# Passages between sub-layers of a two-layer decoder trunk: from the scheduler's order to a written one

## The chip, the cores and the metric

The kernel runs on one core of a Trainium2 chip. The metric is the device time of one execution in microseconds (us). TensorE (PE) multiplies matrices, VectorE (DVE) and ScalarE (ACT) do the work per element, GpSimd (POOL) only small powers here, and SyncE (SP) issues the transfers from the chip's memory.

## The reference, cut to what matters

Two layers; in each a mixing sub-layer and a channel sub-layer on x of 256 tokens by 1024 columns, in f32:

```
mod = silu(c) @ w_ada + b_ada            # shift, scale, gate for both sub-layers
h   = rmsnorm(x) * (1 + scale1) + shift1
q,k,v (two attentions), gate_A, gate_B = split(h @ w_in)
y   = (sigmoid(gate_A) * W_oA(swa(q,k,v)) + sigmoid(gate_B) * W_oB(moba(q,k,v))) @ w_out
x   = x + gate1 * y
h   = rmsnorm(x) * (1 + scale2) + shift2
x   = x + gate2 * (relu(h @ w_up)**2 @ w_down)      # 1024 -> 4096 -> 1024
```

## The kernel before, in words

**Three products for one.** Every f32 operand is split into a high part (a cast to the matrix engine's fp32r format) and a low part (the rest), and every product is three: high by high, high by low, low by high (L523, L524, L525 where the weights are streamed, L528 to L530 where they stand still). A product here is one instruction of 128x128 by 512 columns.

**Weights.** `Stream` (from L387) loads pieces of 2x1024 columns into three raw buffers (`wraw`), ahead of time and in the order of use. Each half of a piece is split into one of eight slots (four `w`, and `ahi`, `alo`, `qT`, `kv`, which attention uses at other times): ACT casts the high part (L441), DVE subtracts it for the low part (L447). A slot comes free when its last product is issued. `fill` splits into every free slot; `stream.hold` stops ordinary splits; with the word "later" the cast is issued and the subtraction kept on a list.

**Sums for the conditioning.** `mod` is not a product on PE: DVE adds up rows of `w_ada` (L257, L260, tile `ada`; 140 long additions L260 in all) as work in the background that `tick()` lets forward a step at a time.

**A passage** lies between two sub-layers. There are three: mixing to channel in layer 0 (near 204 us), channel of layer 0 to mixing of layer 1 (near 392 us), mixing to channel in layer 1 (near 564 us). `out_product` holds its last two blocks of columns back: 48 products, which are then done in four quarters of twelve, token tile t by column half h, so that each quarter of the sum is complete early. A quarter's sum goes through `residual` on DVE (L660 times the gate, L661 onto `x_sb`). When both halves of a token tile are there, `ln_stats` forms the norm: ACT squares and sums (L542, two instructions and a read of the sum each), DVE adds (L545, `lnr`), POOL takes the power (L546), DVE scales x by it (L553, two halves, tile `ln`). `ln_apply(t, h)` then takes four of the eight 128-column blocks: PE transposes them (L571), ACT and DVE each scale and shift two (L578, L581), DVE and ACT round to the high part (L588, L590), DVE subtracts for the low part (L591, two instructions). In the text, half (t, h) is such a half of a token tile.

**After the passage's products**, `proj_first` computes the first 512 columns of the next projection, for token tile 0 and then tile 1, from four weight slots in order, six products each: slots one and two take half (t, 0), slots three and four half (t, 1). The next work is the rest of that projection, or in the channel sub-layer the up-products (L633, L637) with `uhi` and `ulo` (L1253, L1259) as the split of the activated rows.

**The order.** The tile framework's scheduler decides where on each engine an instruction stands, within its data dependences; `tc.issue_after` adds edges, which `stream.behind` uses to put weight splits behind the last `ln_apply`. A block under `tc.manual_schedule()` keeps the written order instead. The lead of layer 0 already uses it. Names with a number are one allocation of a buffer.

Of the kernel before, what the change touches and what calls it, by code (L numbers as in the profile page):

```python
# [8 lines left out]
F32 = mybir.dt.float32  # L9
# [9 lines left out]
DEPTH = 2  # L19
# [42 lines left out]
HOLD = 2  # L62
PAIR_TICKS = 3
ROPE_LAG = 3
XN_ACT = ()
G_LAG = 2
PACE = 2
SM_ACT = ((0, 1, 2, 3), (3,))
# [11 lines left out]
def kernel(ctx: ExitStack, tc: tile.TileContext, io):  # L80
# [102 lines left out]
    def run(g):  # L183
        for _ in g:
            pass
# [204 lines left out]
    class Stream:  # L390
# [58 lines left out]
            if h == 1:  # L449
                self.load_next()  # L450

        def fill(self):
            n = -1
            while n != self.split:
                n = self.split
                self.split_next()

# [205 lines left out]
    def out_product(n, us, make, n0, lsub, after):  # L663
# [16 lines left out]
                held += [(f, k) for k in range(2)]  # L680
        while slow:
            run(slow.pop(0))
        stream.fill()
        stream.hold = True
        halves = []
        for t in range(NT):
            for h in range(2):
                for i, (f, k) in enumerate(held):
                    if t == 0 and h == 0:
                        halves.append(stream.get())  # L690
                    while us[f][2][0] > 0:
                        tick()
                    out_half(accs, halves[i], *us[f], k, f == 0 and k == 0, i == len(held) - 1, (t,), (h,))
                    if t == 0 and h == 0:
                        tick()
                    if t == 1 and h == 1:
                        stream.release(halves[i][0])
                    if i == 1:
                        after(t, h, 0, lambda: residual(accs, gt[l][sub], t, h))
                after(t, h, 1, lambda: residual(accs, gt[l][sub], t, h))  # L700

    def boundary(l, sub):

        chains = {}

        def apply(t, h):
            return ln_apply(l, sub, t, h)

        def after(t, h, part, res):
            if part == 0:  # L710
                if (t, h) == (1, 0):
                    run(chains[0])
                elif (t, h) == (1, 1):
                    apply(0, 0)
                return
            res()
            if h == 0:
                chains[t] = ln_stats(t, XN_ACT)
            next(chains[t])
            if (t, h) == (1, 1):  # L720
                apply(0, 1)

        def finish():
            apply(1, 0)
            return apply(1, 1)

        def rest():
            run(chains[1])

        return after, rest, finish  # L730

    def proj_first(rest, finish):

        ps = [acc_t() for _ in range(NT)]
        rest()
        halves = []
        for t in range(NT):
            ts = slice(t * P, (t + 1) * P)
            for i in range(4):
# [6 lines left out]
                if t == 1:  # L746
                    stream.release(slot)
                    tick()
                elif i == 2:
                    stream.behind = finish()  # L750
                    stream.hold = False
        return ps


    rq = {}
# [169 lines left out]
    def lead():  # L925
# [74 lines left out]
        def cast():  # L1000
            stream.split_next("later")

        def low():
            lo, raw, hi = stream.later.pop(0)
            V.tensor_tensor(out=lo, in0=raw, in1=hi.bitcast(F32), op=ALU.subtract)

        def apply(q, cols):

# [73 lines left out]
        stream.hold = False  # L1082
        return groups, tabs

    def mixing(l, rest, finish):
        done = set()

# [4 lines left out]
        if l == 0:  # L1092
            with tc.manual_schedule():
                (qb, kb, vb), tabs = lead()
        else:
            stream.retire(["qT", "kv"])
            tabs = rope_tables(l)
            qb = proj_first(rest, finish)
        qT = state.tile([P, 8, S], F32, tag="qT", name=nm("qT"), bufs=1)
        kv = state.tile([P, 6 * S + NT * 10 * HD], F32, tag="kv", name=nm("kv"), bufs=1)  # L1100
# [112 lines left out]
    def mlp(l, rest, finish, new_u):  # L1213
# [19 lines left out]
        def up_tokens(ps, us):  # L1233
# [22 lines left out]
            for f in range(2):  # L1256
# [3 lines left out]
                                            in1=us[f][0][:, :, ts].bitcast(F32), op=ALU.subtract)  # L1260
                us[f][2][0] = 0

        pace[0] = 0
        slow.extend(ada_unit(u) for u in ADA_PLAN[2 * l + 1])
        us = [new_u(), new_u()]
        ps = proj_first(rest, finish)
        bg.append(up_tokens(ps, us))
        if l < DEPTH - 1:
            after, rest, finish = boundary(l + 1, 0)
# [55 lines left out]
```

## Time and profile before

| what | value |
|---|---|
| runs of the kernel | 754.0, 754.44, 750.03 us (median 754.0) |
| the profiled execution, its own time | 751.9 us |
| its span, first to last instruction | 750.1 us (the other 1.8 us lie around it) |
| busy share PE / DVE / ACT / POOL | 98% / 80% / 60% / 4% |
| PE's share of the chain that ended last | 85%; DVE 7%, DMA 4%, ACT 2% |
| mean granted clock of TensorE | 0.991 of full speed |

The page gives each engine's busy time over the span; the timelines list instructions by start time, with the time before that the engine stood idle and what ended it in brackets. PE's records of neighbouring products overlap (0.39 us long, 0.23 us apart), so the distance between starts is what a product costs, and an idle time in brackets is counted from the modelled end of the one before. The windows give the busy time of each engine in a stretch, and the granted clock as a share of 2.4 GHz.

### The profile page before, as it was taken

Reading aid. Unit: us, or ns where it says so; the run is one execution under the profiler, and the core shown is the slowest. Engines: PE = TensorE matmul, PEld = TensorE weight load, DVE = VectorE, ACT = ScalarE, POOL = GpSimd, SP = SyncE. Lnnn points to the kernel's source line nnn. Section 1 sums busy time; section 2 is a strip of 40 time slices with the busy share of each in tenths; the row PEclk is TensorE's granted clock in tenths of the full one; section 3 lists DMA queues with packets and bytes.
Section 4 is the critical chain, followed back from the end, with each engine's and each line's share of the span. In section 5 each row is a group of like instructions: output and inputs, shape, how many; then the busy total and the mean of one; then the engine's idle time right before and its main releaser. Section 6 shows DMA issues by size and latency. Waiting matters only on the chain.

```text
span 750.1 us, 11462 instructions
## 1 busy us (share of the span) xinstructions
PE 731.9 (98%) x4265; PEld 626.3 (83%) x4265; DVE 602.1 (80%) x1130; ACT 451.6 (60%) x873; POOL 32.5 (4%) x24
## 2 busy tenths in 40 slices
PE   7999998999899999999999999999999999999997
PEld 6778887899778888888887888889988888888886
DVE  6589998699889899999989879896879865555643
ACT  6545598953466665665546367676446856656650
POOL 1003010000000000000000601000000000000000
PEclk9899999999989999999999999999999999999999
DMA  8987676767828999998883743845561856565511
GB/s 289 392 294 268 226 242 235 254 240 255 280 77 300 318 361 332 345 384 281 333 306 124 244 141 113 262 161 174 195 237 59 292 186 207 170 206 186 180 46 56
DMA packets 110535, 173.41 MB, mean 231 GB/s; under 512 B 4744, under 2 KB 68488, under 8 KB 110480
## 3 DMA queue, kind: packets, MB, share of 16 engines
q1 hardware_dynamic: 109744, 172.54, 68.1%
q8 instruction: 33, 0.54, 0.3%
q10 hardware_dynamic: 736, 0.15, 0.1%
q14 instruction: 22, 0.18, 0.1%
HBM read 171.62 MB, written 1.05 MB: 230 GB/s over the span
## 4 chain that ended last, share of the span: by engine, by line
PE 85%; DVE 7%; DMA 4%; ACT 2%; issue 1%; SPq 0%; POOL 0%; ACTq 0%; DVEq 0%; POOLq 0%
PE tmp L633 14%; PE acc L523 12%; PE acc L525 12%; PE acc L524 12%; PE tmp L637 7%; PE tmp L528 5%; PE tmp L530 5%; PE tmp L529 5%; PE acc L1028 3%; PE acc L851 2%; PE tmp L914 2%; DVE w L447 1%; DVE ada L260 1%; PE tmp L1028 1%; DMA araw<-in_w_ada_dram 1%
## 5 line engine op out<-in xcount | busy, mean ns | idle before, releaser
L441 ACT CAST w<-wraw 128x1024 fp32r<-128x1024 f32 x150 | 155.7, 1048 | 77.4 <-PE acc L525 31.7
L447 DVE TENSOR_TENSOR w<-wraw,w 128x1024 fp32r<-128x1024 f32 x137 | 166.3, 1222 | 37.3 <-ACT w L441 36.4
L260 DVE SCALAR_TENSOR_TENSOR ada<-araw,cs,ada 128x512 f32<-128x512 f32 x140 | 104.6, 747 | 3.2 <-DMA araw<-in_w_ada_dram 2.7
L528 PE MATMUL tmp<-hT,w 128*128 128x256 f32 x256 | 76.8, 300 | 2.5 <-DVE alo L918 2.5
L523 PE MATMUL acc<-w,uhi 128*128 128x512 f32 x192 | 75.3, 392 | 0.0
L524 PE MATMUL acc<-w,uhi 128*128 128x512 f32 x192 | 74.9, 390 | 0.0
L525 PE MATMUL acc<-w,ulo 128*128 128x512 f32 x192 | 74.8, 390 | 0.0
L530 PE MATMUL tmp<-hT,w 128*128 128x256 f32 x256 | 72.4, 283 | 0.0
L529 PE MATMUL tmp<-hT,w 128*128 128x256 f32 x256 | 72.3, 282 | 0.0
L642 ACT COPY usum<-tmp 128x256 f32<-128x256 f32 x56 | 20.8, 371 | 61.1 <-PE tmp L637 61.0
L528 PEld LDWEIGHTS tmp<-hT,w 128*128 128x128 f32 x256 | 48.6, 190 | 9.4 <-issue 5.3
L633 PE MATMUL tmp<-hT,w 128*128 128x512 f32 x224 | 56.4, 393 | 0.0
L530 PEld LDWEIGHTS tmp<-hT,w 128*128 128x128 f32 x256 | 48.7, 190 | 0.7 <-DVE ro L824 0.3
L529 PEld LDWEIGHTS tmp<-hT,w 128*128 128x128 f32 x256 | 48.7, 190 | 0.3 <-issue 0.2
L633 PEld LDWEIGHTS tmp<-hT,w 128*128 128x128 f32 x224 | 41.0, 188 | 7.8
L644 DVE TENSOR_TENSOR usum<-tmp,usum 128x256 f32<-128x256 f32 x56 | 23.7, 422 | 25.5 <-ACT usum L642 25.4
L525 PEld LDWEIGHTS acc<-w,ulo 128*128 128x128 f32 x192 | 36.1, 188 | 7.6
L523 PEld LDWEIGHTS acc<-w,uhi 128*128 128x128 f32 x192 | 36.1, 188 | 7.0
L524 PEld LDWEIGHTS acc<-w,uhi 128*128 128x128 f32 x192 | 36.1, 188 | 6.9
L441 ACT CAST kv<-wraw 128x1024 fp32r<-128x1024 f32 x21 | 22.1, 1053 | 18.7 <-PE acc L525 15.9
L447 DVE TENSOR_TENSOR kv<-wraw,kv 128x1024 fp32r<-128x1024 f32 x21 | 25.6, 1221 | 9.0 <-ACT kv L441 9.0
L637 PEld LDWEIGHTS tmp<-hT,w 128*128 128x128 f32 x224 | 30.6, 190 | 2.2
(250 smaller groups left out, 1760.7 us busy)
## 6 DMA issues: line engine op xcount, KB each, us to landing
araw<-in_w_ada_dram SPq DMA_DIRECT2D x80, 512.0 KB, 5.2
wraw<-in_w_up_dram SPq DMA_DIRECT2D x32, 1024.0 KB, 5.8
wraw<-in_w_down_dram SPq DMA_DIRECT2D x32, 1024.0 KB, 7.0
wraw<-in_w_in_dram SPq DMA_DIRECT2D x28, 1024.0 KB, 6.2
wraw<-in_w_out_dram SPq DMA_DIRECT2D x8, 1024.0 KB, 6.2
wraw<-in_w_in_dram SPq DMA_DIRECT2D x12, 512.0 KB, 7.1
wraw<-in_w_o_swa_dram SPq DMA_DIRECT2D x8, 512.0 KB, 3.5
wraw<-in_w_o_moba_dram SPq DMA_DIRECT2D x8, 512.0 KB, 5.4
```

The source lines that it names most:

```text
L260: nc.vector.scalar_tensor_tensor(out=acc, in0=raw[:, k, :], scalar=cs[:, kk:kk + 1], in1=(bz if kk == 0 else acc), op0=ALU.mult, op1=ALU.add)
L441: nc.scalar.copy(hi, r)
L447: ins = nc.vector.tensor_tensor(out=lo, in0=r, in1=hi.bitcast(F32), op=ALU.subtract)
L523: nc.tensor.matmul(ps, lhsT=lh, rhs=rh, start=start, stop=False)
L524: nc.tensor.matmul(ps, lhsT=lh, rhs=rl, start=False, stop=False)
L525: nc.tensor.matmul(ps, lhsT=ll, rhs=rh, start=False, stop=stop)
L528: nc.tensor.matmul(ps, lhsT=wh, rhs=ah, start=start, stop=False)
L529: nc.tensor.matmul(ps, lhsT=wh, rhs=al, start=False, stop=False)
L530: nc.tensor.matmul(ps, lhsT=wl, rhs=ah, start=False, stop=stop)
L633: nc.tensor.matmul(ps, lhsT=hi[:, k, :], rhs=hT[:, k].rearrange("p a s -> p (a s)"), start=k == 0, stop=False)
L637: nc.tensor.matmul(ps[:, :S], lhsT=lo[:, k, :], rhs=hT_hi[:, k, :], start=False, stop=k == KT - 1)
L1028: T.matmul(ps[t], lhsT=left[:, 2 * q + k, t * P:(t + 1) * P], rhs=w[:, k, :], start=(first and k == 0), stop=(last and k == 1))
```

## The change

One constant now sends the second half of the scaling of x by the norm to ACT, in all passages (`XN_ACT`, the branch of `ln_stats` that was there unused). The held products of `out_product` move to `out_held`, and these and the first 512 columns (`proj_ordered`) are issued in two blocks with manual order, one behind the other. In the first, `fill(2)` leaves two slots, which are then filled at written places: casts by `split_next("later")`, subtractions by `stream.low()`. The residual of quarter (1,0) is written behind `apply(0, 0)`. The products of layer 1's rope tables (`rope_tables`) move from the head of layer 1 to behind the first 512 columns of layer 0's channel sub-layer. The last `out_product` of the kernel stays with the scheduler.

```diff
-XN_ACT = ()
+XN_ACT = (1,)
...
-        def fill(self):
+        def low(self):
+            lo, r, hi = self.later.pop(0)
+            nc.vector.tensor_tensor(out=lo, in0=r, in1=hi.bitcast(F32), op=ALU.subtract)
+
+        def fill(self, keep=0):
             n = -1
-            while n != self.split:
+            while n != self.split and len(self.free) > keep:
...
-        stream.fill()
-        stream.hold = True
+        if lsub == (DEPTH - 1, 1):
+            stream.fill()
+            stream.hold = True
+            out_held(accs, us, held, lsub, after)
+        else:
+            with tc.manual_schedule():
+                stream.behind = None
+                stream.fill(2)
+                stream.hold = True
+                out_held(accs, us, held, lsub, after)
...
-                        after(t, h, 0, lambda: residual(accs, gt[l][sub], t, h))
-                after(t, h, 1, lambda: residual(accs, gt[l][sub], t, h))
+                        after(t, h, 0, None)
+                after(t, h, 1, lambda t=t, h=h: residual(accs, gt[l][sub], t, h))
...
                 if (t, h) == (1, 0):
                     run(chains[0])
+                    stream.low()
                 elif (t, h) == (1, 1):
                     apply(0, 0)
+                    sums.pop()()
+                    next(chains[1])
+                return
+            if h == 0:
+                chains[t] = ln_stats(t, XN_ACT)
+            if (t, h) == (1, 0):
+                sums.append(res)
                 return
             res()
-            if h == 0:
-                chains[t] = ln_stats(t, XN_ACT)
+            if (t, h) == (0, 1):
+                stream.low()
             next(chains[t])
+            if t == 0:
+                stream.split_next("later")
             if (t, h) == (1, 1):
                 apply(0, 1)
...
-    def proj_first(rest, finish):
+    def proj_first(rest, finish, then=lambda: None):
+        with tc.manual_schedule():
+            ps, behind = proj_ordered(rest, finish)
+            then()
+        stream.behind = behind
+        return ps
...
-            tabs = rope_tables(l)
+            tabs = next_tabs.pop()
...
+        def tables():
+            next_tabs.append(rope_tables(l + 1))
...
-        ps = proj_first(rest, finish)
+        ps = proj_first(rest, finish, tables if l < DEPTH - 1 else lambda: None)
```

The lines behind the edit move: residual L660/L661 becomes L665/L666, the square L547, `lnr` L550, the scaling by the norm L556 on ACT and L558 on DVE, transposes L576, scale and shift L583 (ACT) and L586 (DVE), rounding L593 (DVE) and L595 (ACT), low part L596, products L528 to L530; the subtraction written inside is L455.

What this does to the engines' order is shown at three places.

**PE, passage at 204 us**: the end of the held products, the transposes of token tile 0, the start of the first slot. Before:

```order
L525 MATMUL acc_2008<-w_12_2256,ulo_2154 128x512
L523 MATMUL acc_2008<-w_12_2259,uhi_2153 128x512
L524 MATMUL acc_2008<-w_12_2259,uhi_2153 128x512
L525 MATMUL acc_2008<-w_12_2259,ulo_2154 128x512
L571 MATMUL tmp_2342<-cpack,ln_2295 128x128 x2
L571 MATMUL tmp_2345<-cpack,ln_2295 128x128 x2
L571 MATMUL tmp_2366<-cpack,ln_2295 128x128 x2
L571 MATMUL tmp_2369<-cpack,ln_2295 128x128 x2
L523 MATMUL acc_2384<-ahi_2264,hT 128x512
L524 MATMUL acc_2384<-ahi_2264,hT 128x512
```

After:

```order
L529 MATMUL acc_2008<-w_11_2235,uhi_2009 128x512
L530 MATMUL acc_2008<-w_11_2235,ulo_2010 128x512
L576 MATMUL tmp_2339<-cpack,ln_2289 128x128 x2
L576 MATMUL tmp_2342<-cpack,ln_2289 128x128 x2
L528 MATMUL acc_2008<-w_12_2256,uhi_2153 128x512
L529 MATMUL acc_2008<-w_12_2256,uhi_2153 128x512
L530 MATMUL acc_2008<-w_12_2256,ulo_2154 128x512
L528 MATMUL acc_2008<-w_12_2261,uhi_2153 128x512
L529 MATMUL acc_2008<-w_12_2261,uhi_2153 128x512
L530 MATMUL acc_2008<-w_12_2261,ulo_2154 128x512
L576 MATMUL tmp_2368<-cpack,ln_2289 128x128 x2
L576 MATMUL tmp_2371<-cpack,ln_2289 128x128 x2
```

The transposes of half (0,0) stood behind all 48 products and now stand behind 42; the passages at 392 and 564 us had them behind 45 and 42 and now both have 42.

**DVE, passage at 564 us**: from the copies of half (0,0) to those of half (0,1). Before:

```order
L660 TENSOR_TENSOR res_6029<-acc_5735,gt_4779 128x512
L661 TENSOR_TENSOR x_sb<-x_sb,res_6029 128x512
L581 TENSOR_SCALAR ln_5993<-tmp_6043,s_1_1_100,sh_1_104 128x128 x2
L588 CAST hT<-ln_5993 128x2x128
L591 TENSOR_TENSOR hT<-ln_5993,hT 128x2x128
L660 TENSOR_TENSOR res_6060<-acc_5736,gt_4779 128x512
L591 TENSOR_TENSOR hT<-ln_5993,hT 128x2x128
L661 TENSOR_TENSOR x_sb<-x_sb,res_6060 128x512
L581 TENSOR_SCALAR ln_5993<-tmp_6067,s_1_1_100,sh_1_104 128x128 x2
L588 CAST hT<-ln_5993 128x2x128
L545 TENSOR_SCALAR lnr_6084<-lnv_6032 128x1
L591 TENSOR_TENSOR hT<-ln_5993,hT 128x2x128 x2
```

After:

```order
L586 TENSOR_SCALAR ln_5999<-tmp_6052,s_1_1_100,sh_1_104 128x128 x2
L593 CAST hT<-ln_5999 128x2x128
L596 TENSOR_TENSOR hT<-ln_5999,hT 128x2x128 x2
L665 TENSOR_TENSOR res_6063<-acc_5747,gt_4791 128x512
L666 TENSOR_TENSOR x_sb<-x_sb,res_6063 128x512
L665 TENSOR_TENSOR res_6074<-acc_5748,gt_4791 128x512
L666 TENSOR_TENSOR x_sb<-x_sb,res_6074 128x512
L586 TENSOR_SCALAR ln_5999<-tmp_6081,s_1_1_100,sh_1_104 128x128 x2
L550 TENSOR_SCALAR lnr_6101<-lnv_6066 128x1
L558 TENSOR_SCALAR ln_5999<-x_sb,lnr_6101 128x512
L593 CAST hT<-ln_5999 128x2x128
L596 TENSOR_TENSOR hT<-ln_5999,hT 128x2x128 x2
```

Both residuals of tile 1 (L665, L666) now stand between the copies of half (0,0) and the scaling of half (0,1), and `lnr` and the scaling of tile 1 (L550, L558) stand ahead of half (0,1)'s rounding (L593). The passage at 204 us reads the same. On ACT both squares of tile 1 stand ahead of the scaling of half (0,1); before, the scaling stood between the two squares.

**DVE, passage at 392 us**, from the copies of half (0,0) on. Before:

```order
L581 TENSOR_SCALAR ln_4089<-tmp_4139,s_1_0_99,sh_0_103 128x128 x2
L588 CAST hT<-ln_4089 128x2x128
L660 TENSOR_TENSOR res_4156<-acc_2487,gt_2594 128x512
L591 TENSOR_TENSOR hT<-ln_4089,hT 128x2x128 x2
L661 TENSOR_TENSOR x_sb<-x_sb,res_4156 128x512
L581 TENSOR_SCALAR ln_4089<-tmp_4163,s_1_0_99,sh_0_103 128x128 x2
L588 CAST hT<-ln_4089 128x2x128
L545 TENSOR_SCALAR lnr_4186<-lnv_4128 128x1
L591 TENSOR_TENSOR hT<-ln_4089,hT 128x2x128 x2
L553 TENSOR_SCALAR ln_4089<-x_sb,lnr_4186 128x512 x2
L260 SCALAR_TENSOR_TENSOR ada_4925<-araw_4679,cs,ada_4925 128x512
L260 SCALAR_TENSOR_TENSOR ada_4925<-araw_4926,cs,ada_4925 128x512
```

After:

```order
L260 SCALAR_TENSOR_TENSOR ada_4569<-araw_4603,cs,ada_4569 128x512
L596 TENSOR_TENSOR hT<-ln_4099,hT 128x2x128 x2
L665 TENSOR_TENSOR res_4163<-acc_2502,gt_2610 128x512
L260 SCALAR_TENSOR_TENSOR ada_4569<-araw_4603,cs,ada_4569 128x512
L666 TENSOR_TENSOR x_sb<-x_sb,res_4163 128x512
L665 TENSOR_TENSOR res_4174<-acc_2503,gt_2610 128x512
L260 SCALAR_TENSOR_TENSOR ada_4937<-araw_4643,cs,bz 128x512
L666 TENSOR_TENSOR x_sb<-x_sb,res_4174 128x512
L586 TENSOR_SCALAR ln_4099<-tmp_4181,s_1_0_99,sh_0_103 128x128 x2
L260 SCALAR_TENSOR_TENSOR ada_4937<-araw_4643,cs,ada_4937 128x512
L550 TENSOR_SCALAR lnr_4197<-lnv_4166 128x1
L593 CAST hT<-ln_4099 128x2x128
```

Four sums for the conditioning (L260) stand in this piece where none stood up to the rounding of half (0,1). In the whole passage there are 12, two of them ahead of the scaling of tile 0 by the norm (L558) and five behind the rounding of half (0,1); before there were five. In the other two passages none is left: 7 follow the passage's last copy at 204 us, together with four weight splits, the eight rope products and four roundings, ahead of the first `ulo`; 7 and four splits do at 564 us, from sums that stood in layer 1's attention before.

## Rows read from the trace of the kernel before

**Rows 1.** The page: busy us, share of span, instructions by engine.

```profile
PE 731.9 (98%) x4265; PEld 626.3 (83%) x4265; DVE 602.1 (80%) x1130; ACT 451.6 (60%) x873; POOL 32.5 (4%) x24
```

**Rows 2.** Windows: stretch, length, busy us by engine, granted clock, DMA share, GB/s.

```profile
204.00:216.00 12.00, 8.37 (x28) 6.16 (x27) 9.71 (x24) 4.37 (x12) 1.48 (x2) 0.72 0.43 131
...
225.00:375.00 150.00, 150.00 (x780) 128.30 (x779) 141.63 (x215) 93.55 (x165) 0.00 (x0) 1.00 0.94 332
...
100.00:125.00 25.00, 22.14 (x176) 19.34 (x176) 22.14 (x63) 21.97 (x64) 0.00 (x0) 1.00 0.70 233
```

**Rows 3.** Timeline of PE, passage at 204 us: start, us, line, tiles [idle before].

```profile
203.90 0.39 PE L525 MATMUL acc<-w,ulo 128*128 128x512 f32 x1
207.18 1.09 PE L571 MATMUL tmp<-cpack,ln 128*128 128x128 f32 x8 [2.90 <-DVE ln L553]
...
209.61 0.63 PE L524 MATMUL acc<-ahi,hT 128*128 128x512 f32 x1
...
214.81 0.51 PE L524 MATMUL acc<-qT,hT 128*128 128x512 f32 x1
...
216.10 1.04 PE L571 MATMUL tmp<-cpack,ln 128*128 128x128 f32 x8
```

**Rows 4.** Timeline of PE, passage at 392 us.

```profile
393.78 0.39 PE L525 MATMUL acc<-w,ulo 128*128 128x512 f32 x1
...
398.66 0.39 PE L524 MATMUL acc<-alo,hT 128*128 128x512 f32 x1
```

**Rows 5.** Timeline of PE, passage at 564 us.

```profile
563.78 0.40 PE L525 MATMUL acc<-w,ulo 128*128 128x512 f32 x1
...
570.76 1.04 PE L571 MATMUL tmp<-cpack,ln 128*128 128x128 f32 x8
```

**Rows 6.** Timeline of DVE, passage at 564 us.

```profile
560.85 0.69 DVE L661 TENSOR_TENSOR x_sb<-x_sb,res 128x512 f32<-128x512 f32 x1
...
564.08 0.69 DVE L660 TENSOR_TENSOR res<-acc,gt 128x512 f32<-128x512 f32 x1
564.80 0.69 DVE L661 TENSOR_TENSOR x_sb<-x_sb,res 128x512 f32<-128x512 f32 x1
565.41 0.72 DVE L581 TENSOR_SCALAR ln<-tmp,s,sh 128x128 f32<-128x128 f32 x2
...
566.71 0.68 DVE L660 TENSOR_TENSOR res<-acc,gt 128x512 f32<-128x512 f32 x1
...
569.12 0.22 DVE L545 TENSOR_SCALAR lnr<-lnv 128x1 f32<-128x1 f32 x1
...
570.12 0.88 DVE L553 TENSOR_SCALAR ln<-x_sb,lnr 128x512 f32<-128x512 f32 x2
```

**Rows 7.** Timeline of ACT, passage at 564 us: the last square.

```profile
568.36 0.63 ACT L542 ACTIVATE ln<-x_sb 128x512 f32<-128x512 f32 x1 [1.08 <-DVE x_sb L661]
```

**Rows 8.** Timeline of DVE elsewhere: one sum, three weight splits.

```profile
386.60 0.75 DVE L260 SCALAR_TENSOR_TENSOR ada<-araw,cs,ada 128x512 f32<-128x512 f32 x1
...
220.54 3.49 DVE L447 TENSOR_TENSOR w<-wraw,w 128x1024 fp32r<-128x1024 f32 x3
```

**Rows 9.** The line of the rope products: ns min/median/max, start times, forms.

```profile
L384 DVE TENSOR_TENSOR ct<-gqk,sincos x8: 285/288/291, 38.0 to 112.2; 128x128 f32<-128x128 f32 x8
```

**Rows 10.** Timeline of PE: first product with `ulo`, layer 0 and layer 1.

```profile
230.70 0.39 PE L525 MATMUL acc<-w,ulo 128*128 128x512 f32 x1
...
585.37 0.39 PE L525 MATMUL acc<-w,ulo 128*128 128x512 f32 x1
```

**Rows 11.** Timeline of DVE and PE: a sum that waits for its transfer.

```profile
115.38 0.75 DVE L260 SCALAR_TENSOR_TENSOR ada<-araw,cs,ada 128x512 f32<-128x512 f32 x1 [2.66 <-DMA araw<-in_w_ada_dram]
...
117.66 0.39 PE L528 MATMUL tmp<-hT,w 128*128 128x256 f32 x1 [2.52 <-DVE alo L918]
```

**Rows 12.** Timeline of POOL: powers of the norm at 393 and 563 us.

```profile
393.12 0.87 POOL L546 TENSOR_TENSOR lnr<-lnr,mhalf 128x1 f32<-128x1 f32 x1 [181.17 <-DVE lnr L545]
...
562.70 0.56 POOL L546 TENSOR_TENSOR lnr<-lnr,mhalf 128x1 f32<-128x1 f32 x1 [97.82 <-DVE lnr L545]
```

More of the change, by code (lines that the diff above doesn't have):

```diff
@@ L682, in out_product, with out_held @@
             run(slow.pop(0))
-        stream.fill()
-        stream.hold = True
+        if lsub == (DEPTH - 1, 1):
[8 more added lines that the diff above has]
+                out_held(accs, us, held, lsub, after)
+    def out_held(accs, us, held, lsub, after):
+        l, sub = lsub
         halves = []
@@ L698, in out_product @@
                     if i == 1:
-                        after(t, h, 0, lambda: residual(accs, gt[l][sub], t, h))
-                after(t, h, 1, lambda: residual(accs, gt[l][sub], t, h))
+                        after(t, h, 0, None)
+                after(t, h, 1, lambda t=t, h=h: residual(accs, gt[l][sub], t, h))
     def boundary(l, sub):
         chains = {}
+        sums = []
         def apply(t, h):
@@ L730, in boundary, with proj_ordered @@
         return after, rest, finish
-    def proj_first(rest, finish):
+    def proj_first(rest, finish, then=lambda: None):
[4 more added lines that the diff above has]
+        return ps
+    def proj_ordered(rest, finish):
         ps = [acc_t() for _ in range(NT)]
@@ L749, in proj_first @@
                 elif i == 2:
-                    stream.behind = finish()
+                    behind = finish()
                     stream.hold = False
-        return ps
+        return ps, behind
     rq = {}
@@ L1001, in cast @@
             stream.split_next("later")
-        def low():
-            lo, raw, hi = stream.later.pop(0)
-            V.tensor_tensor(out=lo, in0=raw, in1=hi.bitcast(F32), op=ALU.subtract)
+        low = stream.low
         def apply(q, cols):
@@ L1083, in lead @@
         return groups, tabs
+    next_tabs = []
     def mixing(l, rest, finish):
```

## The prediction

> **What bounds the kernel.** First the page's line of engines: PE is busy 98% of the span [rows 1], so only what PE stands still in, or runs slowly in, can be won. Then the windows: layer 0's channel stage has PE busy for all of its 150 us at clock 1.00, with DVE close behind at 141.6 us, while the 12 us of the first passage show PE busy 8.4 us at clock 0.72 [rows 2]. So I measured the three passages on PE's timeline: the distance of two starts less what lies between at full speed, 0.227 us per product (12 x 0.227 = 2.72 us for a quarter) and 0.109 us per transpose.
>
> - 204 us: from 203.90 to 216.10 stand 19 products and 8 transposes, 4.31 + 0.87 = 5.18 us of work in 12.20: **7.0 lost**. 2.90 of it is the wait for tile 0's norm. Another 2.5 is the clock: between 209.61 and 214.81 twelve products take 0.433 us each, 12 x (0.433 - 0.227), right after that wait [rows 3].
> - 392 us: from 393.78 to 398.66 stand 11 products and 8 transposes, 3.37 us of work in 4.88: **1.5 lost** [rows 4].
> - 564 us: from 563.78 to 570.76 stand 25 products and 8 transposes, 6.55 us in 6.98: **0.4 lost** [rows 5].
>
> All that the change can win there is 8.9 us. What it does is in the order, and so in the chain on DVE that feeds PE.
>
> **Part 1: the chain of the passage at 564 us.** It has no sums in it, so the rows give every spacing: a gate product to its addition 0.72 and the addition to the next 0.61 [rows 6], two scalings with rounding and a first low part 1.30 (565.41 to 566.71), the second low part 0.33 (estimate, its neighbour's spacing), a weight subtraction (3.49 - 1.22)/2 = 1.135 [rows 8]. From the last square's start to `lnr` 0.76 and from `lnr` over the power to the scaling by the norm 1.00 [rows 6, 7].
>
> Count forward from the addition at 560.85 that completes tile 0. A weight subtraction at 561.46 now stands ahead of `lnr`, which comes at 562.60 (562.34 before), the scaling of tile 0 at 563.56; its second half is on ACT beside it. PE reaches the transposes at 564.0 as before and finds them 0.1 late. The second weight subtraction keeps DVE to 565.09. Then the copies of half (0,0), 1.30 + 0.33, to 566.71; the two residuals of tile 1, 0.72 + 0.60 + 0.72 + 0.69, to 569.44. ACT's last square follows, `lnr` at 570.24, the scaling by the norm at 571.24 for 0.40, and only then the rounding of half (0,1), 571.65, done and seen by PE at **571.99**.
>
> PE meanwhile does the other 6 held products, 4 transposes and the 12 products of slots one and two: it stands before slot three at 564.1 + 0.44 + 1.36 + 0.44 + 2.72 = **569.06**. The wait is 2.93. Of this, 0.9 is the detour over `lnr` and the norm; with the rounding ahead of these the wait would be 2.0. Total lost 0.1 + 2.9 + 0.1 for the rest = 3.1 against 0.4: **+2.7** (bounds +1.6 without the detour, +2.9).
>
> **Part 2: the passage at 204 us** gets the same order and chain. There the transposes behind 42 products instead of 48 keep PE busy while the norm is made, and the wait of 2.90 shrinks; I take 0.5 (bounds 0.1, as at 564 us, and 2.9, nothing gained). Behind it the same 2.9 at slot three. 3.6 lost against 7.0: **-3.4** at the end of the first 512 columns, if the clock holds.
>
> What becomes of it: DVE ends its copies some 3.2 us before PE ends these columns, at 217.1 (PE 220.3, before 223.8). Then, ahead of the first `ulo`, stand 7 sums at 0.66 (0.75 less the 0.09 by which neighbours overlap), 4 weight subtractions, the 8 rope products at 0.20 (0.29 less 0.09), four roundings and a sum, 4.6 + 4.5 + 1.6 + 1.1 = 11.9 us [rows 8, 9], so that `ulo` is there at 217.1 + 11.9 + 0.4 = 229.45. PE would want it at 230.70 - 3.4 = 227.3 [rows 10]. 2.2 us are given back: **-1.2** (bounds -3.4, nothing given back, and 0). DVE's 8 us of slack in the next 150 [rows 2] absorb its lateness there.
>
> Where the rope products and the layer-1 sums came from nothing is won: the rope products stood before 112.5, and DVE then sat idle 2.66 us for a sum's transfer [rows 11].
>
> **Part 3: the passage at 392 us** has the same chain with sums between. Two stand ahead of the scaling of tile 0, 1.3 us in all, and PE waits about 0.9 for the transposes (bounds 0.1 and 1.3) and 0.3 for the low part. Four more stand up to the rounding of half (0,1), which here comes ahead of the norm of tile 1: 2.0 + 4 x 0.66, less the 1.1 by which PE is later itself = 3.5 at slot three (bounds 2.0 and 4.6). Behind it five sums, 3.3 us, lie between the copies of tile 1; about half reach PE, 1.5 (bounds 0 and 3.3). 6.2 lost against 1.5: **+4.7** (bounds +2.6, if sums keep out of the way, and +6).
>
> The power on POOL that lies in this chain took 0.87 us at 393.12, beside DVE work, and 0.56 at 562.70 with DVE idle [rows 12]; a sum now stands beside it, so 0.87 is in the 0.9. The Trainium skill, "SBUF — State Buffer", section "Who interferes with whom", says that a DVE instruction with two inputs in that memory contends with a POOL instruction that reads it, and that the later one is fully blocked. By that rule the power could take 0.56 + 0.69 = 1.25 us and the sum be 761.6; the trace agrees in direction, with 0.31 more and not 0.69, and the sum goes by the rows.
>
> **Part 4: the tail at 564 us.** After its last copy at 577.9 DVE now has 7 sums, 4 weight subtractions, roundings and a sum, 10.3 us, and `ulo` comes at 588.65. PE wants it at 585.37 + 2.7 = 588.1 [rows 10]: **+0.6** (bounds 0 and 1).
>
> **Part 5: the clock.** Three waits of 2.9 to 3.5 us stand where one of 2.90 stood. That one was followed by 2.5 us lost at half clock [rows 3]; the one of 2.52 at 117.66 by none, its window shows 1.00 [rows 2, 11]. At 204 us a fall would vanish in the 2.2 us that PE waits for `ulo` anyhow. Of the other two I take the longer, at 392 us, to cost **+2.5** (bounds 0 and 5.0 for both).
>
> **Sum**: the profiled execution took 751.9 us, its span 750.1. 751.9 - 1.2 + 4.7 + 2.7 + 0.6 + 2.5 = 761.2, so **761 us**. That profile stands 2.1 us under the median of 754.0; against the median the forecast is +0.9%, just inside 1%, which is about what a measurement of this kernel can tell from no change (its runs spread over 0.6%).
>
> **The rivals.**
>
> *The waits without the clock*: the same chain, and no fall: 758.7 us, no change. For it, the 2.52-us wait; against it, that both waits are longer. With falls at both, 763.7, slower. I give this mechanism 0.66 in all: 0.22 none, 0.27 one (761), 0.17 both.
>
> *The written order works*: slot three's rounding comes within the 12 products, by 569.06, since DVE runs ahead of what I count, and each passage loses 0.4 like the one at 564 us now. 751.9 - (8.9 - 1.2) = 744.2, faster by 1.3%. It is decided at the residuals of tile 1: they cost DVE 2.73 us between the two halves' copies, where PE has 2.72 us of products, before the square, the scaling and the rounding. For it, that the passage at 564 us does as well now with the same work; against it, that there one residual stood ahead of half (0,0) and the scaling ahead of the last square. 0.08.
>
> *Only the first passage counts*: the first passage keeps its 3.4, the sums at 392 us stay in DVE's idle gaps, no tail and no clock: 751.9 - 3.4 + 2.6 + 1.6 = 752.7, no change. 0.16.
>
> *A sum waits for its transfer in the passage at 392 us*: the sums there consume pieces whose buffers come free only as earlier sums pass, and in a written order everything behind a late one stands still; the price is in the rows, 2.66 us [rows 11]. 763.7 + 2.7 = 766.4, slower. 0.10.
>
> The order is not wholly as written, either: the two blocks mix (the norm of tile 1, from the second, ahead of a rounding of the first), and sums stand within the block at 392 us. That is in the forecast.
>
> The range, 752 to 767, leaves out the 744 case and what lies beyond the bounds at 392 us. Faster by over 1%: 0.08. Slower: both falls and the late transfer, 0.27, and half of the 761 case, which lies on the line, 0.13: 0.40. Within 1%: the rest, 0.52.
>
> **What the profile after would show.** Right: PE idle before slot three (L528 of the third slot) 2.5 to 3.5 us in each passage, released by DVE's rounding L593; the wait of 2.90 for the norm at 204 us gone, and a wait for `ulo` of about 2 us behind it; sums between the copies at 392 us; PE's clock below 1.00 after at least one of these waits. Wrong: no wait at slot three, or one under 1 us, which would mean that DVE or ACT works in another order or at another pace than counted; a full clock throughout (759); a gain at 204 us beyond 3.4.

## The result and the profile after

The changed kernel took 761.04, 762.57, 761.56 and 758.8 us, median 761.3; the kernel before, on the same chip, 754.0, 754.44, 750.03 and 749.55, median 752.0. The ratio is 1.0127, 95% interval 1.0089 to 1.0164: slower by 1.3%; the prediction had given 0.40 to slower by over 1% and 0.52 to a change within 1%. The profiled execution of the changed kernel took 761.04 us, 9.1 more than that of before.

The page of the changed kernel, its span and the line of engines (beside [rows 1]):

```profile
span 759.0 us, 11446 instructions
...
PE 733.7 (97%) x4265; PEld 627.4 (83%) x4265; DVE 599.9 (79%) x1124; ACT 456.8 (60%) x879; POOL 31.0 (4%) x24
```

PE is busy 1.8 us longer, DVE 2.2 us shorter, in a span 8.9 us longer: PE stands still more. Its three largest waits between 90 and 620 us, the stretch of the passages (what PE waited for, us in total, times, longest):

```profile
PE acc L528 <- DVE hT L593: 8.4, 3, 3.3
PE tmp L533 <- DVE alo L954: 2.5, 1, 2.5
PE tmp L576 <- DVE ln L558: 0.9, 1, 0.9
```

The first line is new, 8.4 us in three waits: the third weight slot of each passage for the rounding of half (0,1). The second was there before ([rows 11], 2.52). The wait of 2.90 for the norm at 204 us [rows 3] is gone.

PE's timeline of the first passage, to be laid beside [rows 3]:

```profile
205.44 0.39 PE L530 MATMUL acc<-w,ulo 128*128 128x512 f32 x1
205.87 0.66 PE L576 MATMUL tmp<-cpack,ln 128*128 128x128 f32 x4
...
210.73 0.39 PE L530 MATMUL acc<-alo,hT 128*128 128x512 f32 x1
213.72 0.50 PE L528 MATMUL acc<-qT,hT 128*128 128x512 f32 x1 [2.60 <-DVE hT L593]
...
215.24 0.63 PE L530 MATMUL acc<-qT,hT 128*128 128x512 f32 x1
215.66 1.91 PE L576 MATMUL tmp<-cpack,ln 128*128 128x128 f32 x8
217.22 0.77 PE L528 MATMUL acc<-kv,hT 128*128 128x512 f32 x1
```

The transposes follow the 42nd product after 0.43, 0.2 late. Behind slot two comes the wait, 2.60, and soon after it products take 0.43 and eight transposes 1.56 us from start to start: half clock, 1.2 GHz, where a product at full clock takes 0.23. The passage at 564 us has the same wait and keeps the full clock (the last product of slot two, the first of slot three, the next):

```profile
574.98 0.39 PE L530 MATMUL acc<-alo,hT 128*128 128x512 f32 x1
577.93 0.50 PE L528 MATMUL acc<-qT,hT 128*128 128x512 f32 x1 [2.56 <-DVE hT L593]
578.26 0.40 PE L529 MATMUL acc<-qT,hT 128*128 128x512 f32 x1
```

DVE there shows the chain that the prediction counted, beside [rows 6]:

```profile
566.98 0.69 DVE L666 TENSOR_TENSOR x_sb<-x_sb,res 128x512 f32<-128x512 f32 x1
567.59 1.22 DVE L455 TENSOR_TENSOR qT<-wraw,qT 128x1024 fp32r<-128x1024 f32 x1
568.72 0.20 DVE L550 TENSOR_SCALAR lnr<-lnv 128x1 f32<-128x1 f32 x1
569.60 0.49 DVE L558 TENSOR_SCALAR ln<-x_sb,lnr 128x512 f32<-128x512 f32 x1 [0.67 <-POOL lnr L551]
570.00 1.22 DVE L455 TENSOR_TENSOR kv<-wraw,kv 128x1024 fp32r<-128x1024 f32 x1
571.13 0.72 DVE L586 TENSOR_SCALAR ln<-tmp,s,sh 128x128 f32<-128x128 f32 x2
...
572.77 0.69 DVE L665 TENSOR_TENSOR res<-acc,gt 128x512 f32<-128x512 f32 x1
...
574.82 0.69 DVE L666 TENSOR_TENSOR x_sb<-x_sb,res 128x512 f32<-128x512 f32 x1
575.43 0.72 DVE L586 TENSOR_SCALAR ln<-tmp,s,sh 128x128 f32<-128x128 f32 x2
576.30 0.21 DVE L550 TENSOR_SCALAR lnr<-lnv 128x1 f32<-128x1 f32 x1
577.18 0.48 DVE L558 TENSOR_SCALAR ln<-x_sb,lnr 128x512 f32<-128x512 f32 x1 [0.67 <-POOL lnr L551]
577.59 0.28 DVE L593 CAST hT<-ln 128x256 fp32r<-128x256 f32 x1
```

From the addition to the end of the last residual it has one gap, 0.67 us for the power; then the scaling of half (0,1), `lnr`, another 0.67 for the power, the scaling by the norm and only then the rounding (577.59). Counted from the addition, the rounding was forecast at 571.65 - 560.85 = 10.80 us and came at 10.61.

In the passage at 392 us the sums stand in that chain. DVE up to the rounding and behind it:

```profile
397.88 0.74 DVE L260 SCALAR_TENSOR_TENSOR ada<-araw,cs,ada 128x512 f32<-128x512 f32 x1
...
399.81 0.74 DVE L260 SCALAR_TENSOR_TENSOR ada<-araw,cs,ada 128x512 f32<-128x512 f32 x1
...
401.68 0.74 DVE L260 SCALAR_TENSOR_TENSOR ada<-araw,cs,bz 128x512 f32<-128x512 f32 x1
...
403.58 0.74 DVE L260 SCALAR_TENSOR_TENSOR ada<-araw,cs,ada 128x512 f32<-128x512 f32 x1
404.24 0.20 DVE L550 TENSOR_SCALAR lnr<-lnv 128x1 f32<-128x1 f32 x1
404.50 0.29 DVE L593 CAST hT<-ln 128x256 fp32r<-128x256 f32 x1
404.71 0.74 DVE L260 SCALAR_TENSOR_TENSOR ada<-araw,cs,ada 128x512 f32<-128x512 f32 x1
405.37 0.76 DVE L596 TENSOR_TENSOR hT<-ln,hT 128x256 fp32r<-128x256 f32 x2
406.04 0.48 DVE L558 TENSOR_SCALAR ln<-x_sb,lnr 128x512 f32<-128x512 f32 x1
406.44 2.32 DVE L260 SCALAR_TENSOR_TENSOR ada<-araw,cs,ada 128x512 f32<-128x512 f32 x3
```

And PE's timeline there, the start of slot three:

```profile
404.85 0.50 PE L528 MATMUL acc<-qT,hT 128*128 128x512 f32 x1 [3.27 <-DVE hT L593]
...
405.85 0.79 PE L530 MATMUL acc<-qT,hT 128*128 128x512 f32 x1 [0.27 <-DVE hT L596]
```

Slot three waits 3.27 us, with four sums from the copies of half (0,0) up to its rounding. To see where time went, two starts of PE's timeline are taken per passage: S, the start of the first of the last twelve held products, and E, the start of the last product of the first 512 columns. Between them lie 59 products and 16 transposes, 15.12 us at full speed (59 x 0.2267 + 16 x 0.109); the rest is lost. Both kernels were profiled a second time for this (the first two experiments below).

| us | before | after | before, again | after, again |
|---|---|---|---|---|
| start to S at 204 us | 201.41 | 204.30 | 203.59 | 203.56 |
| lost at 204 us | 7.05 | 4.90 | 6.60 | 5.08 |
| E to S at 392 us | 168.39 | 169.39 | 168.39 | 169.50 |
| lost at 392 us | 1.75 | 7.14 | 1.74 | 6.72 |
| E to S at 564 us | 153.81 | 152.81 | 153.81 | 152.80 |
| lost at 564 us | 0.47 | 3.00 | 0.49 | 4.62 |
| E to the end of PE's last product | 167.57 | 167.83 | 167.57 | 168.07 |

In the first pair the changed kernel enters its first passage 2.89 us late, which no part of the forecast had; in the second pair it does not (-0.03). The rest of the difference in span is +6.0 in the first pair and +8.2 in the second: -1.15 and -0.41 for the first passage with the stage behind it, +5.39 and +4.98 at 392 us, -1.00 and -1.01 in layer 1's mixing, +2.53 and +4.13 at 564 us, +0.26 and +0.50 behind it.

### The profile page after: what moved, and what is told of

It is laid out like the page before. It is cut to its first block, busy times and chain, and to the rows that moved or that the text cites. A ratio compares the mean times of both kernels' runs of the same rounds, so it can differ in the third digit from the quotient of the medians.

```text
span 759.0 us, 11446 instructions
## 1 busy us (share of the span) xinstructions
PE 733.7 (97%) x4265; PEld 627.4 (83%) x4265; DVE 599.9 (79%) x1124; ACT 456.8 (60%) x879; POOL 31.0 (4%) x24
## 4 chain that ended last, share of the span: by engine, by line
PE 76%; DVE 11%; DMA 7%; issue 3%; ACT 2%; POOL 0%; ACTq 0%; SPq 0%; POOLq 0%; DVEq 0%
PE tmp L638 12%; PE acc L530 11%; PE acc L528 11%; PE acc L529 11%; PE tmp L642 6%; PE tmp L533 6%; PE tmp L535 5%; PE tmp L534 5%; DVE ada L260 2%; PE acc L887 2%; PE tmp L950 2%; DMA wraw<-in_w_in_dram 2%; PE acc L1062 1%; DVE w L447 1%; DMA kv<-in_w_ada_dram 1%
## 5 line engine op out<-in xcount | busy, mean ns | idle before, releaser
L260 DVE SCALAR_TENSOR_TENSOR ada<-araw,cs,ada 128x512 f32<-128x512 f32 x140 | 104.2, 745 | 4.6 <-DMA araw<-in_w_ada_dram 4.1
L533 PE MATMUL tmp<-hT,w 128*128 128x256 f32 x256 | 78.2, 305 | 2.5 <-DVE alo L954 2.5
L528 PE MATMUL acc<-w,uhi 128*128 128x512 f32 x192 | 75.4, 393 | 0.0
L530 PE MATMUL acc<-w,ulo 128*128 128x512 f32 x192 | 74.5, 390 | 0.0
L535 PE MATMUL tmp<-hT,w 128*128 128x256 f32 x256 | 73.6, 287 | 0.0
L534 PE MATMUL tmp<-hT,w 128*128 128x256 f32 x256 | 73.5, 287 | 0.0
L533 PEld LDWEIGHTS tmp<-hT,w 128*128 128x128 f32 x256 | 49.9, 195 | 9.6 <-issue 5.5
L535 PEld LDWEIGHTS tmp<-hT,w 128*128 128x128 f32 x256 | 50.0, 195 | 0.7 <-issue 0.3
L534 PEld LDWEIGHTS tmp<-hT,w 128*128 128x128 f32 x256 | 50.2, 196 | 0.2
L638 PEld LDWEIGHTS tmp<-hT,w 128*128 128x128 f32 x224 | 41.0, 188 | 7.8
L530 PEld LDWEIGHTS acc<-w,ulo 128*128 128x128 f32 x192 | 36.0, 188 | 8.2 <-DVE ulo L1295 0.6
L528 PEld LDWEIGHTS acc<-w,uhi 128*128 128x128 f32 x192 | 36.1, 188 | 6.8
L642 PEld LDWEIGHTS tmp<-hT,w 128*128 128x128 f32 x224 | 30.6, 190 | 2.2
L642 PE MATMUL tmp<-hT,w 128*128 128x256 f32 x224 | 31.2, 282 | 0.0
L819 POOL TENSOR_TENSOR rs<-ss,mhalf 128x16 f32<-128x16 f32 (+1 forms) x8 | 24.7, 3091 | 127.5 <-DVE ss L818 71.4
```

The source lines that it names most:

```text
L260: nc.vector.scalar_tensor_tensor(out=acc, in0=raw[:, k, :], scalar=cs[:, kk:kk + 1], in1=(bz if kk == 0 else acc), op0=ALU.mult, op1=ALU.add)
L528: nc.tensor.matmul(ps, lhsT=lh, rhs=rh, start=start, stop=False)
L530: nc.tensor.matmul(ps, lhsT=ll, rhs=rh, start=False, stop=stop)
L533: nc.tensor.matmul(ps, lhsT=wh, rhs=ah, start=start, stop=False)
L534: nc.tensor.matmul(ps, lhsT=wh, rhs=al, start=False, stop=False)
L535: nc.tensor.matmul(ps, lhsT=wl, rhs=ah, start=False, stop=stop)
```

## The experiments

Losses below are those of the table, in the three passages in order.

**Both kernels again**, unedited.

> The kernel before, once more. Theory (waits of the chain on DVE make the difference): the three passages lose 7.0, 1.5 and 0.4 us again, within 0.3, and the time lies in 749.5 to 754.5. Rival (the difference is one of the clock): the stretches at half clock, which lay in the first 50 us (0.93) and in 204 to 216 us (0.72), lie elsewhere this time; if 112 to 125 us shows a clock under 0.9 here too, the 2.9 us that the changed kernel is late ahead of its first passage are not of the change.

> The changed kernel, once more. Theory: the waits ahead of the third weight slot (L528 for L593) come back at 2.6, 3.3 and 2.6 us within 0.1, since they follow from the order on DVE; time 758 to 763. Rival (clock): those waits stay and the half clock in 112 to 125 us (0.64) is gone or has another length; then its place is a matter of the execution. If it is there again at 0.64, the change has a part in it.

One execution each: 753.67 us and 761.98 us; the kernel before, timed beside these two and the next two, took 755.45. The window of 112 to 125 us (columns as in [rows 2]) of the kernel before in its second profile; in the first the clock was 1.00 from 100 to 125 us [rows 2]:

```profile
112.00:125.00 13.00, 10.95 (x61) 8.57 (x60) 7.95 (x23) 7.70 (x22) 0.00 (x0) 0.74 0.55 181
```

The same window of the changed kernel, first profile:

```profile
112.00:125.00 13.00, 10.52 (x51) 8.14 (x50) 7.35 (x19) 6.29 (x19) 0.00 (x0) 0.64 0.42 142
```

And its second profile:

```profile
112.00:125.00 13.00, 10.33 (x56) 7.95 (x55) 7.35 (x19) 6.77 (x20) 0.00 (x0) 0.74 0.50 162
```

The kernel before has a half-clock stretch there too in its second execution, and it differs from itself by 2.2 us ahead of its first passage. The traces of the experiments below tell more: up to 3 us before S, PE, ACT and DVE issue the same instructions in the same order in `after`, `after_again`, `res_early`, `sums_out` and `lnr_copies`, and S at the first passage lies at 204.30, 203.56, 199.99, 199.41 and 204.51 us. A spread of 5.1 us stands in one and the same order, so 2.9 us there need no change of the kernel. The waits at slot three came back as 2.62, 3.27 and 2.54, and this time the one at 564 us was followed by half clock as well (4.62 lost in place of 3.00).

**The residual back ahead of the copies** (`res_early`).

```diff
                 elif (t, h) == (1, 1):
                     apply(0, 0)
-                    sums.pop()()
-                    next(chains[1])
...
-            if (t, h) == (1, 0):
-                sums.append(res)
-                return
             res()
```

> The residual of quarter (1,0) back in front of the copies of half (0,0). Theory (DVE is busy without a gap from the second written split to the last residual, so order within it only moves the wait): a new wait of about 1.0 us ahead of the first weight slot in the passages at 204 and 564 us, the one ahead of the third slot down from 2.6 by about 1.0, the sum and the time unchanged within 1 us. Rival (the deferral itself is the cost): no wait at the first slot and the third slot's wait down by 1.3, the time 3 to 4 us less. Other rival (one wait is as good as another for the clock): half clock less often, since the waits are shorter.

One execution, 756.14 us; lost 4.15, 7.30 and 3.95, at clock 1.00 in all three passages. The wait moved, as expected, but the loss rose by 0.9 at 564 us. ACT's timeline there:

```profile
567.13 0.63 ACT L547 ACTIVATE ln<-x_sb 128x512 f32<-128x512 f32 x1 [2.26 <-DVE x_sb L666]
...
567.76 0.79 ACT L583 ACTIVATE ln<-tmp,sh,s 128x128 f32<-128x128 f32 x2
```

DVE's:

```profile
568.58 0.29 DVE L593 CAST hT<-ln 128x256 fp32r<-128x256 f32 x1 [0.84 <-ACT ln L583]
```

And PE's, slots one and three:

```profile
568.93 0.50 PE L528 MATMUL acc<-ahi,hT 128*128 128x512 f32 x1 [1.76 <-DVE hT L593]
...
573.42 0.50 PE L528 MATMUL acc<-qT,hT 128*128 128x512 f32 x1 [1.49 <-DVE hT L593]
```

With the residual goes the square of tile 1, and ACT now does it (567.13) ahead of scaling half (0,0) (567.76), so DVE stands 0.84 us and slot one waits 1.76. I had held the chain to be DVE's alone; it has a leg on ACT, and keeping the square behind it is what the change's deferral does. The rival with the deferral as the cost fell: there is a wait at the first slot. The other rival, half clock less often with shorter waits, came true in this one profile, though a wait of 2.62 at 392 us stands in it. The time is 5.8 us under that of the changed kernel beside it, of which 3.6 lie ahead of the first passage (S at 199.99 and 203.56).

**The same with all splits ahead of the block** (`full_early`).

```diff
-                stream.fill(2)
+                stream.fill()
...
-                    stream.low()
...
-            if (t, h) == (0, 1):
-                stream.low()
             next(chains[t])
-            if t == 0:
-                stream.split_next("later")
```

> As the last, and all weight splits ahead of the block again (fill into every slot, none written inside). Theory: at 564 us, where the splits' data are there early, two subtractions of 1.135 us leave the chain; the third slot's wait falls to about 1.6 and the passage loses 1.7 instead of 3.1; at 204 us, where the data come late, both subtractions now stand ahead of the first residuals and PE waits some 4 us for the transposes, 2 us more lost than in the changed kernel. Rival (the order of the residual and the copies is what counts, the splits are covered): both passages as in the last kernel. Time about the same in both.

One execution, 753.59 us; lost 5.16 (clock 0.92 there), 4.37 and 2.54. At 564 us slot one waits 0.42 where it waited 1.76 in `res_early`, still for the square, and slot three 1.48 as there (1.49); 2.54 is more than the 1.7 expected by the wait at slot one and less than 3.00. At 204 us the transposes wait 2.14, the side expected, at half the size, but slot three only 0.81, so the 2 us more that were expected there did not come (5.16 against 4.90 and 5.08). So where data come early the written splits lengthen the chain. The time equals that of the kernel before only because the first passage begins 4.0 us earlier (S at 199.56 against 203.59); by the parts of the table this kernel stands 3.7 us above the second profile of the kernel before, `res_early` 6.0 and the changed kernel 8.2.

**No sums in the passage at 392 us** (`sums_out`).

```diff
-ADA_PLAN = (range(4, 10), range(10, 20), range(20, 22), range(22, 24))
+ADA_PLAN = (range(4, 10), range(10, 17), range(17, 22), range(22, 24))
```

> Of the sums for the conditioning three units (17 to 19) move from layer 0's channel stage to layer 1's mixing stage, so that none stands within the passage at 392 us; the written order is untouched. Theory (the sums in the chain cost what they take): that passage becomes a copy of the one at 564 us; waits 0.1 for the transposes, 2.6 ahead of the third slot, none behind; it loses 3.1 instead of 6.2 at full clock, and the kernel about 3 us, 758 against 761. Rival (sums lie in gaps of the chain and cost nothing): waits stay at 0.9 and 3.3, time unchanged.

757.54 us, ratio to before 1.0100 (1.0065 to 1.0135); lost 6.28, 4.63 and 4.61 at clock 0.84, 0.91 and 0.91. At 392 us the waits of 0.91 and 0.27 are gone and slot three's is that of the other passages:

```profile
398.01 0.50 PE L528 MATMUL acc<-qT,hT 128*128 128x512 f32 x1 [2.46 <-DVE hT L593]
```

The mechanism stands: without the sums this passage waits as the others do. The gain of 2.5 us there was given back in layer 1's mixing, E to S 155.29 against 152.81: 12 PE instructions moved with the three units, and PE waited 0.8 for their columns. Whether the kernel is faster than the changed one the intervals leave open.

**The rounding ahead of the norm** (`lnr_copies`).

```diff
             if (t, h) == (1, 1):
+                next(chains[1])
                 apply(0, 1)
+                run(chains[1])
```

> The norm of tile 1 is written into the first block: lnr, then the copies of half (0,1), then the scaling by the norm. Theory: the detour of the rounding over the power and the scaling (about 0.9 of the wait) goes; the third slot's wait falls from 2.6 to 2.0 us at 204 and 564 us, nothing at 392 us, where the rounding stood ahead already; time 1 to 1.5 us less. Rival (the wait moves to the transposes of tile 1, whose norm is now later): a new wait there of 0.6, time unchanged.

760.32 us, ratio 1.0136 (1.0084 to 1.0189); lost 4.18, 7.33 and 2.47. The third slot at 564 us:

```profile
577.25 0.50 PE L528 MATMUL acc<-qT,hT 128*128 128x512 f32 x1 [2.04 <-DVE hT L593]
```

2.04 instead of 2.56, and 2.03 at 204 us, no wait at tile 1's transposes: the detour was 0.5 to 0.6, not 0.9. The likely reason, not tested alone: the rounding needs ACT's half of the scaled blocks as well (the wait of 0.84 in `res_early`), and in the changed kernel ACT scales them only behind the last square, up to 576.96, 0.63 ahead of the rounding at 577.59:

```profile
576.17 0.79 ACT L583 ACTIVATE ln<-tmp,sh,s 128x128 f32<-128x128 f32 x2
```

At 392 us slot three waits 3.90, since one more sum slipped ahead of the rounding, five in place of four. The passages lose 1.1 us less in all than in the first profile of the changed kernel, which is under what the timing resolves.

**The constant alone** (`xn_alone`), on the kernel before.

```diff
-XN_ACT = ()
+XN_ACT = (1,)
```

> The kernel before, with the one constant of the change (second half of the scaling by the norm on ACT) and the scheduler's order. Theory: it gives 0.4 us of DVE per tile and passage and takes nothing; time within 1 us of before, passage losses within 0.5 of 7.0, 1.5 and 0.4. Rival (the constant is what slows the passages): the passages at 392 and 564 us lose 1 us more each.

Ratio 1.0007 (0.9983 to 1.0032); lost 7.07, 1.52 and 0.92. It does nothing that the timing can tell from no change.

**Written order in the first passage only** (`first_only`; the constant too applies there alone, and `plain` holds the lines of the kernel before).

```diff
-        if lsub == (DEPTH - 1, 1):
+        if lsub != (0, 0):
...
-        with tc.manual_schedule():
+        with tc.manual_schedule() if manual else ExitStack():
...
         def after(t, h, part, res):
+            if (l, sub) != (0, 1):
+                return plain(t, h, part, res)
```

> The written order and the constant in the passage at 204 us alone; the other two are left to the scheduler as before; the rope products stay where the change put them. Theory: the passage at 204 us as in the changed kernel (loses 3.6 at full clock, 2.6 ahead of the third slot), of the gain about 1 us left at the first ulo product, the passages at 392 and 564 us at 1.5 and 0.4 lost; time 750.5 to 753, 8 us under the changed kernel and level with before or 1 us under it. Rival (what is lost lies ahead of the first passage, as the 2.9 us there suggest): the first passage enters 2.9 us late here too, and the time is 754 or more.

Ratio 1.0017 (0.9987 to 1.0047), level with before; lost 5.38, 1.31 and 0.46, clock 0.92 in the first. So the loss comes with the written order of the other two passages. E to S at 392 us is 169.57, 1.2 over before, so of the first passage's 1.7 us 0.5 is left.

**And without the crowd ahead of the first `ulo`** (`first_tail`; `first_best` also has the edit of `lnr_copies`). As `first_only`; in addition the sums of layer 0's channel stage are issued behind the last subtraction of the first `ulo` (`ada_gate`), two units of them move to layer 1, and the rope products are back at the head of layer 1.

```diff
-ADA_PLAN = (range(4, 10), range(10, 20), range(20, 22), range(22, 24))
+ADA_PLAN = (range(4, 10), range(10, 18), range(18, 22), range(22, 24))
...
-            tabs = next_tabs.pop()
+            tabs = rope_tables(l)
...
-        slow.extend(ada_unit(u) for u in ADA_PLAN[2 * l + 1])
...
+            ada_gate[0] = low_ins.ins if l == 0 else None
+            slow.extend(ada_unit(u) for u in ADA_PLAN[2 * l + 1])
```

> As the kernel with only the first passage in written order; in addition the sums of layer 0's channel stage start behind its first ulo (an edge to the last ulo subtraction), two units of them move to layer 1, and the rope products are back at the head of layer 1. Theory (the gain at 204 us is given back at the first ulo, since DVE has 7 sums and 8 rope products ahead of it): no wait there, 3.4 us gained at 204 us are kept, no sums at 392 us, so that passage loses under 1; time 747 to 749, 0.5% under before. Rival (DVE is too busy in the next 150 us to be late by 6 us): a wait appears later in the channel stage and the time is 751 or more.

> As the last, with lnr, copies of half (0,1), scaling by the norm in this order in the first passage. Theory: another 0.6 us off the third slot's wait at 204 us; 746.5 to 748.5, and the fastest of all. Rival: no difference to the last, as the norm of tile 1 is later by as much.

Medians of 12 runs 748.94 and 748.9 (before 750.35); ratios 0.9981 (0.9949 to 1.0012) and 0.9969 (0.9939 to 0.9999). PE in the changed kernel: the first and the last of the products with `uhi` ahead of the first with `ulo`, and the one place behind these where it stands still before the next passage:

```profile
230.98 0.40 PE L528 MATMUL acc<-w,uhi 128*128 128x512 f32 x1
...
232.60 0.39 PE L529 MATMUL acc<-w,uhi 128*128 128x512 f32 x1
233.02 1.21 PE L530 MATMUL acc<-w,ulo 128*128 128x512 f32 x4
...
255.28 0.40 PE L275 MATMUL tmp<-ghi,ones 128*128 128x512 f32 x1
256.11 0.50 PE L276 MATMUL tmp<-glo,ones 128*128 128x512 f32 x1 [0.43 <-DVE glo L272]
```

And the first product with `ulo` in `first_tail`:

```profile
229.22 0.39 PE L538 MATMUL acc<-w,ulo 128*128 128x512 f32 x1
```

From E it is 8.70 us in the changed kernel (224.32), 7.13 in `first_tail` (222.09) and 7.13 in the kernel before (223.57 to 230.70 [rows 10]). So `ulo` is 1.57 late in the changed kernel, but PE does not stand still for that long. Eight products with `uhi` go ahead of the first with `ulo`, where there are two in the kernel before; the six more fill 1.4 of the 1.57, and by the distances of starts PE loses 0.3 there. It loses another 0.7 at 256.11, for `glo`, the low part of a conditioning sum, which DVE makes behind the crowd. These two make the 1.00 by which E to S at 392 us grew; the second profile has them too (0.4 and 0.8), and the kernel before has neither. In `first_tail` both are gone. E to S at 392 us falls by 2.0 to 167.41, 0.9 of that with 8 PE instructions that moved to layer 1. Losses of `first_tail` are 4.10 (at clock 1.00), 0.42 and 0.46: against before -2.95, -1.33, -0.01 in the passages and -0.98 in the stage behind the first, +0.74 in layer 1's mixing, -4.5 in all by the profiles. The timing shows 1.4 to 2.3, which is just clear of no change for `first_best` alone, whose lower wait (2.04) was followed by half clock in its profile, 4.58 lost.

## Why the prediction was right, point by point

**The chain at slot three** was right in mechanism and size. Forecast 2.9, 3.5 and 2.9 us of wait, measured 2.60, 3.27 and 2.56 by the profile's idle time, and 2.76, 3.44 and 2.72 by the distance of starts, as the forecast counted; lost at 564 us 3.1 forecast, 3.00 measured. From `lnr` to the scaling I took 1.00, and it was 0.88 (576.30 to 577.18). The detour in it was mis-sized: 0.9 forecast, 0.5 by `lnr_copies`, probably since it leaves out ACT's scaling beside it.

**The first passage** came to -1.15 and -0.41 in the two pairs where -1.2 was forecast, but not by the terms forecast. The passage itself was to give 3.4 and gave 2.15 and 1.52: it lost 4.90, some 1.4 of it to half clock and so about 3.5 without, 3.6 forecast. Behind it 2.2 were to be given back by a wait for the first `ulo`, and 1.00 and 1.11 were. That wait, which I had named as a sign of being right, is not there: DVE was late as counted, but PE did six other products first and lost 0.3. The other 0.7 went for `glo` 23 us later, where I had let DVE's slack absorb its lateness. That the net of the first pair meets the forecast is luck: two errors of over 1 us cancel. That the crowd on DVE makes both losses was shown by `first_tail`, where it is moved away.

**The passage at 392 us** came to +5.4 where I had +4.7 and 2.5 for the clock. The term that failed is the 1.5 us for the five sums between the copies of tile 1: the wait there is 0.27 in the profile. The half clock took some 1.5 (three products 0.43 apart, eight transposes in 1.54 us). Whether it hid part of that term is not shown; in `res_early`, at full clock, PE waited 0.11 at the copies of tile 1.

**The clock** was the badly placed term. I gave it 2.5 us at 392 us; it took 1.4 to 1.6 behind each wait that it followed, at 204 and 392 us in both profiles, at 564 us in one of two. The 2.9 us that made the sum come out at the forecast lay ahead of the first passage, and the profiles do not show them to be the change's.

**Wrong in the forecast**: that nothing is won where layer 1's sums came from. Layer 1's mixing runs 1.0 us faster without its 18 sums (E to S at 564 us: 153.81 and 153.82 in three profiles with 16 to 18 sums there, 154.52 with 24, 152.78 to 152.81 in five with two or none). What they cost behind the passage I had counted as 0.6, measured 0.26 and 0.50.

So the forecast of 761 against 761.3 is closer than its parts are, and that is luck: of the 9.3 us forecast the two pairs of profiles show 6.0 and 8.2 behind the start of the first passage, and the stretch ahead of it adds what the execution brings. The timings put the whole at 6.7 to 12.3.

**The power on POOL** took 0.99 us at 394.48 beside a sum and 0.56 at 204.73, 212.38, 569.01 and 576.59, where DVE stood idle:

```profile
204.73 0.56 POOL L551 TENSOR_TENSOR lnr<-lnr,mhalf 128x1 f32<-128x1 f32 x1 [108.68 <-DVE lnr L550]
...
394.48 0.99 POOL L551 TENSOR_TENSOR lnr<-lnr,mhalf 128x1 f32<-128x1 f32 x1 [181.54 <-DVE lnr L550]
```

```profile
394.32 0.74 DVE L260 SCALAR_TENSOR_TENSOR ada<-araw,cs,ada 128x512 f32<-128x512 f32 x1
```

The sum had 0.58 left when the power started, and the power ended 0.41 after the sum did (395.47, 395.06). The rows of both kernels agree on this: all seven powers in the passages that started while a DVE instruction ran ended 0.41 to 0.42 after it, whatever was left of it, 0.59 to 0.99 long. The rule of the Trainium skill ("SBUF — State Buffer", section "Who interferes with whom") that the later of two such instructions is fully blocked agrees with that. The forecast's price for it, 0.56 + 0.69, was too high: it took the whole of the other instruction, and only what was left of it counts.

## What to carry to other kernels

Before writing an order out by hand, count the engine that feeds the passage from its first late input to the output that the bound engine waits for, including the other engine's leg between; if that chain is longer than the products beside it, the written order chooses where the wait stands, and only work taken out of the chain (the sums, the splits) shortens it. The scheduler's mixed order was better in two of three passages, so replace it only where its profile shows a loss, and look at what piles up behind the block: background work kept out of it stands ahead of the next stage's inputs. A product that comes late is not yet a wait: see what the engine did in the meantime.

## What the runs showed of the hardware

The clock after a wait is not a property of the kernel alone. In the passages of the twelve profiles, all four waits of 2.90 to 3.90 us were followed by products or transposes at half clock, waits of 2.03 to 2.66 in 12 of 16 cases, and no wait of 1.76 or less by itself; the same kernel gave both outcomes for the same wait (564 us: 2.56 at a granted clock of 1.00 in the passage, 2.54 at 0.91). A stretch that holds 2.9 us of difference between two profiles should be profiled again before it is explained.
